# Front of a hybrid diffusion step: later small loads, a latent tile begun by token halves, norm weights inside the rotation tables

## The chip, the cores and the metric

One core of a Trainium2 chip runs the whole program in one launch. The metric is the device time of one execution in microseconds (us), lower is better; it is compared as a median of several runs. TensorE (PE) does the matrix products and the transposes, VectorE (DVE) and ScalarE (ACT) the elementwise work, GpSimd (POOL) some elementwise work and some DMA issues, SyncE (SP) the other DMA issues.

## What is computed

The reference is one layer of a trunk with 1024 latent tokens and 256 prompt tokens, D_MODEL = 1024, all in fp32. Cut to the part that the change touches:

```python
mod = silu(cond) @ w_ada + b_ada                  # cond = c for latent tokens, c_ctx for prompt
sh1, sc1, g1, sh2, sc2, g2 = split(mod, 6)
h = rms_norm(x, norm_mix_w) * (1 + sc1) + sh1
z = h @ w_in                                      # hq, hf_f, hf_b, hi, hg, aq, ak, av, gl
q = rms_norm(aq by heads of 64, q_norm_w)         # 8 query heads
k = rms_norm(ak by heads of 64, k_norm_w)         # 2 key heads
if latent:                                        # 2-D axial rotary positions
    q, k = axial_rope(q), axial_rope(k)           # per half: x1*cos - x2*sin, x1*sin + x2*cos
    k, v = concat(cache_k, k), concat(cache_v, v)
# then attention, a gated linear recurrence (HGRN), gates, an output projection, an MLP, norms
```

## The kernel before, in words

**Numbers and tiles.** Every fp32 operand of a product is kept as a pair, a rounded high part and the rest: ACT copies the high part, DVE subtracts (`split`, lines 277 and 278). One product is three matmuls: high by high, high by low, low by high. Tokens are tiled as t=0 and t=1 (512 latent tokens, 4 blocks of 128 each) and t=2 (256 prompt tokens, 2 blocks). The width 1024 is cut into KC=8 chunks kc of 128. A *step* z(t,kc) below is the matmuls of chunk kc for tile t onto the 512 columns of `w_in` that hold k, v and half of the queries (`front_z`, lines 553 to 562): for 4 blocks 8 matmuls with the high part of h (L558, L559), then 4 with its low part (L562).

**The front (lines 577 to 633).** `norm1_rows` (224 to 251) loads the token rows `xr`, takes sums of squares (ACT L241, for t=0 half of them on DVE L237 and L238), raises the mean to the power -0.5 on POOL (`rst`, L247) and scales the rows on DVE (L250). `front_ada(j)` (518 to 534), j=0..3, loads eight 256 KB pieces `wa` of `w_ada` and does 64 narrow matmuls (L530) for the shift and scale columns of two chunks; its result is copied by ACT (`ev`, L533), and `front_late(j)` (536 to 545) transposes it on PE (L539) and makes `modc` and `s` (`s1`) on DVE (L543, L544). `norm1_tr` (253 to 257) transposes the rows of one chunk into a PSUM tile `ps_t`, of which there are two, and `norm1_col` (259 to 271) reads it: ACT makes the high part `hs` (L265), ACT or for every third chunk DVE the unrounded value `xnb` (L270, L268), DVE the low part `hs` (L271). `front_w(kc)` (547 to 551) loads and splits a row block `wst` of `w_in`.

For t=0 the columns come two chunks at a time, between the steps z(0,kc). From step 7 on, columns run AHEAD=3 steps before their step: ahead of z(0,7) stand the 12 transposes of chunks 0 to 2 of t=1.

**What follows a tile.** `front_done` copies the banks out by pairs of blocks (`kve` L442, `qe` L448). `front_prep` calls `kv_consume` and `q_consume` for each pair: `qk_norm` (390 to 416) squares (ACT L394), reduces (DVE L396), adds EPS (DVE L165), takes the power on POOL (`qrst`, L166), multiplies by it (`qn`, DVE L399) and by the norm weight `qwb` or `kwb` (DVE L400). For latent pairs the rotation follows: `qa` = `qn` by `cosb`, one DVE op for each block (L408); `qb` = `qn` with its halves exchanged by `sinb`, two POOL ops for each block (L413); their sum on POOL for queries and DVE for keys (L415). The transposes of rotated keys (`k_stack`, L424) and queries (L473) are put on PE some way behind, by a clock of due times (`DUE`, `due`, `flush`). `cache_kv` does the same for the cached keys and values (`ck`, `cv`). After the front `z_tok(AQ)` multiplies the other half of the queries; its first matmul is L325.

**Order.** The order on PE is that of the program text. On the other engines a scheduler orders the instructions by priority: `norm1_col` and the evacuations have a raised one (`high_priority(offset=600)`). Buffers come from rings: the rows `xr` from ring X of 20, the loads `wa` and `wst` from other rings, and a load waits until its buffer is free.

**Small loads (lines 116 to 149).** `small` loads short vectors as rows and transposes them into `cols` (L129, L130). SP issues `c` and `c_ctx` as its first two; POOL issues the rest at the start: `b_ada`, `norm_mix_w`, `norm_ffn_w`, `final_norm_w`, `hgrn_lb_logits`, `qwb`, `kwb`, `hnb` and two masks.

## Time and profile before

| what | us |
|---|---|
| median of 3 runs (2054.65 to 2057.73) | 2055.32 |
| the profiled execution | 2055.24 |
| its span in the trace | 2053.1 |
| PE busy in the span | 2012.3 |
| DVE busy | 1405.3 |
| ACT busy | 938.5 |
| POOL busy | 546.1 |

The mean granted clock of PE is 0.998 of full. The page's busy times are sums over the whole span; the front is its first 104 us, and the rows that matter are those that a view of this stretch gives: what PE waited for, by line, and the instructions of each engine in order of time. In a row of the timeline stand the start, the duration, the engine, the line, the operation with "out<-in", the shape, the count, and in brackets how long the engine was idle before it and what released it. A group of several instructions in one row has the duration from its first start to its last end.

### The profile page before, as it was taken

The page shows a single profiled execution, that of the slowest core. Times are in us where ns is not written, and L with a number is a line of the kernel's source. Part 1 is how long each engine was busy: PE and PEld are TensorE (multiplying, and loading weights), DVE is VectorE, ACT ScalarE, POOL GpSimd, SP SyncE. Part 2 cuts the span into 40 slices and gives each one's busy share as a digit, 9 for nine tenths or more (in the row PEclk, how much of TensorE's full clock was granted, in tenths as well). Part 3 has the DMA queues.
Part 4 walks back from the last instruction along what each step waited for, and adds up shares of the span by engine and source line. Part 5 has one row for each costly group of instructions (what it writes and reads, how often), then busy time and mean ns, then how long its engine had stood idle before and what let it go on. Part 6 is the DMA issues. An engine that isn't in the chain of part 4 may idle for free.

```text
span 2053.1 us, 33691 instructions
## 1 busy us (share of the span) xinstructions
PE 2012.3 (98%) x12470; PEld 1736.1 (85%) x12470; DVE 1405.3 (68%) x2655; ACT 938.5 (46%) x1906; POOL 546.1 (27%) x566
## 2 busy tenths in 40 slices
PE   6899999999999999999999999999999999999998
PEld 5798889988889988888888889998888888888886
DVE  4876776777776788779254634886666666577686
ACT  4735555555555423332321335655455544333443
POOL 1473333333332265545112101222122110000130
PEclk9999999999999999999999999999999999999999
DMA  9453220322211455455544533864444489455764
GB/s 309 150 187 97 78 77 27 108 86 78 78 45 65 132 175 167 153 173 159 196 138 149 180 113 116 259 186 151 157 147 157 145 292 361 148 159 176 232 238 142
DMA packets 220052, 317.38 MB, mean 155 GB/s; under 512 B 18504, under 2 KB 139168, under 8 KB 219888
## 3 DMA queue, kind: packets, MB, share of 16 engines
q1 hardware_dynamic: 207216, 275.05, 41.7%
q0 software_dynamic: 12672, 40.18, 5.5%
q8 instruction: 98, 1.61, 0.3%
q14 instruction: 66, 0.54, 0.1%
HBM read 229.43 MB, written 85.74 MB: 154 GB/s over the span
## 4 chain that ended last, share of the span: by engine, by line
PE 62%; DVE 2%; issue 1%; ACT 0%; DMA 0%; POOL 0%; POOLq 0%; ACTq 0%; DVEq 0%
PE ps_g L308 5%; PE ps_g L309 5%; PE ps_g L310 5%; PE ps_g L1614 2%; PE ps_g L1616 2%; PE ps_g L1615 2%; PE ps_s L1460 2%; PE ps_s L1461 2%; PE ps_s L1459 2%; PE ps_s L1614 2%; PE ps_s L1615 2%; PE ps_s L1616 2%; PE ps_t L1614 2%; PE ps_t L1615 2%; PE ps_t L1616 2%; PE ps_s L308 2%
## 5 line engine op out<-in xcount | busy, mean ns | idle before, releaser
L308 PE MATMUL ps_g<-hs,wsp 128*128 128x512 f32 (+1 forms) x896 | 322.2, 360 | 1.1 <-DVE adas L186 1.0
L310 PE MATMUL ps_g<-hs,wsp 128*128 128x512 f32 (+1 forms) x896 | 309.3, 345 | 0.0
L309 PE MATMUL ps_g<-hs,wsp 128*128 128x512 f32 (+1 forms) x896 | 309.1, 345 | 0.0
L716 POOL TENSOR_SCALAR pexp<-pexp,rs 128x512 f32<-128x512 f32 (+1 forms) x104 | 171.5, 1655 | 364.8 <-ACT pTh L741 210.6
L277 ACT ACTIVATE wsp<-wraw 128x1024 fp32r<-128x1024 f32 x110 | 109.7, 997 | 276.6 <-PE ps_g L309 82.8
L278 DVE TENSOR_TENSOR wsp<-wraw,wsp 128x1024 fp32r<-128x1024 f32 x110 | 139.9, 1272 | 114.8 <-ACT wsp L277 114.4
L308 PEld LDWEIGHTS ps_g<-hs,wsp 128*128 128x128 f32 x896 | 169.6, 189 | 22.3 <-issue 4.6
L310 PEld LDWEIGHTS ps_g<-hs,wsp 128*128 128x128 f32 x896 | 169.3, 189 | 21.5
L309 PEld LDWEIGHTS ps_g<-hs,wsp 128*128 128x128 f32 x896 | 169.9, 190 | 14.8
L741 ACT ACTIVATE pTh<-ps_t 128x512 fp32r<-128x512 f32 x200 | 118.4, 603 | 124.5 <-PE ps_t L738 124.4
L277 ACT ACTIVATE ah<-ar 128x640 fp32r<-128x640 f32 (+1 forms) x112 | 80.9, 723 | 185.1 <-PE ps_g L1615 102.3
L698 DVE TENSOR_REDUCE mx<-ps_s 128x1 f32<-128x512 f32 (+1 forms) x208 | 137.1, 663 | 37.7 <-PE ps_s L697 36.9
L708 ACT ACTIVATE pexp<-ps_s,ngm 128x512 f32<-128x512 f32 (+1 forms) x208 | 137.4, 670 | 43.7 <-DVE ngm L702 42.9
L278 DVE TENSOR_TENSOR ah<-ar,ah 128x640 fp32r<-128x640 f32 (+1 forms) x112 | 93.1, 832 | 77.2 <-ACT ah L277 76.1
L742 DVE TENSOR_TENSOR pTl<-ps_t,pTh 128x512 fp32r<-128x512 f32 x200 | 135.9, 681 | 14.1 <-ACT pTh L741 13.9
L697 PE MATMUL ps_s<-Kl,Ql 128*128 128x512 f32 (+1 forms) x416 | 130.7, 411 | 0.7 <-ACT pexp L708 0.7
L738 PE MATMUL ps_t<-ident,pexp 128*128 128x128 f32 x800 | 120.8, 273 | 3.3 <-DVE pTl L742 1.8
L325 PE MATMUL ps_g<-wsp,hs 128*128 128x256 f32 x400 | 115.9, 290 | 0.0
L327 PE MATMUL ps_g<-wsp,hs 128*128 128x256 f32 x400 | 112.9, 282 | 0.0
L326 PE MATMUL ps_g<-wsp,hs 128*128 128x256 f32 x400 | 112.5, 281 | 0.0
L754 PE MATMUL ps_g<-pTl,Vl 128*128 128x256 f32 x400 | 105.9, 287 | 4.0 <-DVE pTl L742 4.0
L738 PEld LDWEIGHTS ps_t<-ident,pexp 128*128 128x128 f32 x800 | 93.6, 140 | 14.1 <-issue 4.0
(421 smaller groups left out, 5395.2 us busy)
## 6 DMA issues: line engine op xcount, KB each, us to landing
ar<-AF SPq DMA_DIRECT2D x112, 320.0 KB, 3.2
wraw<-in_w_ff SPq DMA_DIRECT2D x32, 1024.0 KB, 6.1
wr<-in_w_ff SPq DMA_DIRECT2D x128, 256.0 KB, 4.4
wraw<-in_w_in SPq DMA_DIRECT2D x18, 1024.0 KB, 5.7
wraw<-in_w_ada SPq DMA_DIRECT2D x16, 1024.0 KB, 5.6
AF<-a POOLq DMA_DIRECT2D x48, 256.0 KB, 2.7
AF<-t POOLq DMA_DIRECT2D x48, 256.0 KB, 2.4
wa<-in_w_ada SPq DMA_DIRECT2D x32, 256.0 KB, 5.8
```

What stands on the lines that cost most here:

```text
L277: s_.activation(hi, raw, AF.Copy)
L278: return v.tensor_tensor(lo, raw, f32(hi), op=ALU.subtract)
L308: pe.matmul(out, hi[:, k, :], mh, start=(first and k == 0), stop=False)
L309: pe.matmul(out, hi[:, k, :], ml, start=False, stop=False)
L310: pe.matmul(out, lo[:, k, :], mh, start=False, stop=(last and k == kcs - 1))
L697: pe.matmul(pq[:, 0:n], self.qh[:, q0:q0 + P], K[self.g][var][self.kts[i]], start=(var == 0), stop=(var == 1))
L698: v.tensor_reduce(self.mx[j][:, i:i + 1], pq[:, 0:n], axis=AX.X, op=ALU.max)
L708: s_.activation(e[:, 0:n], self.ps.pop((j, i))[:, 0:n], AF.Exp, bias=self.mx[j], accum_out=self.sm[j][:, i:i + 1])
L716: NORM[(i + j) % len(NORM)].tensor_scalar(x, x, self.rs[j], None, op0=ALU.mult)
L738: pe.transpose(pt[:, a, j * P:(j + 1) * P], self.Ps[j][i][:, b * P:(b + 1) * P], ident)
L742: v.tensor_tensor(lo, pt, f32(hi), op=ALU.subtract)
L1614: pe.matmul(bank, ph, wh, start=first and i == 0, stop=False, **more)
```

## The change

1. **Small loads.** `c` and `c_ctx` are issued by POOL, ahead of `b_ada`; SP starts with `xr`. `qwb` and `kwb` are issued by POOL behind the row powers of t=0. `hnb`, the masks and the three vectors that are needed later (`load_rest`) are issued by POOL at step 7, behind the row powers of t=1. The two loads of `state_hgrn` go behind `sinb` on SP.
2. **Row norms by halves.** `norm1_rows` takes a list of blocks: blocks 0,1 and blocks 2,3 have a power each. Half of the squares of every tile (i=1) are one DVE op with an accumulated sum. For t=1 and t=2 the squares are gated behind named instructions (`issue_after`).
3. **First columns.** The 8 transposes of chunks 0 and 1 of t=0 stand inside the 64 matmuls of `front_ada(0)`, ahead of k=6. The splits of the first two row blocks of `w_in` are ordered behind `ev` and the scales.
4. **Tile t=1.** z(0,7) is cut: 8 matmuls, then the transposes of chunks 0 and 1 for blocks 0,1 of t=1, then its last 4. z(1,0) and z(1,1) run for blocks 0,1 first, then the transposes for blocks 2,3, z(1,0) for blocks 2,3, the 12 transposes of chunks 2 to 4, and z(1,1) for blocks 2,3. The evacuation of t=0 is ordered by pairs between these. Later columns run 3 to 5 steps ahead; `cache_kv` comes four steps later.
5. **Rotation.** `rope_tables` makes four tables on POOL with 6 ops, the cosines and sines times the norm weight of queries and of keys. For rotated pairs the multiplication L400 is gone, `qa` is one DVE op and `qb` one POOL op with a reversed axis.

```diff
-    small((("c", 8), ("c_ctx", 8)), CC, sp)()
+    small((("c", 8), ("c_ctx", 8)), CC, g_)()
...
+                    if i == 1:
+                        jk = S(name="sqv")
+                        v.scalar_tensor_tensor(jk, xt[i], 1.0, xt[i], op0=ALU.mult, op1=ALU.mult, accum_out=acc)
...
+    def rope_tables():
+
+        cosq, sinq = S((P, 8, 64), name="cosb"), S((P, 8, 64), name="sinb")
+        for c, sn, w in ((cosq, sinq, qwb), (cosb, sinb, kwb)):
+            g_.tensor_tensor(c, cosb, w.unsqueeze(1).broadcast_to([P, 8, 64]), op=ALU.mult)
...
+            for s in range(2):
+                g_.tensor_tensor(out[:, :, :, s], in_[:, :, :, s], w4[:, :, 1 - s].unsqueeze(1).broadcast_to([P, 8, 2, 16]), op=ALU.mult)
...
-        for bb in range(2):
-            blk = blk0 + bb
-            v.tensor_tensor(qa[:, bb], qn[:, bb], cosb[:, blk].unsqueeze(1).broadcast_to([P, nh, 64]), op=ALU.mult)
...
-            for s in range(2):
-                g_.tensor_tensor(bv[:, :, :, s], nv[:, :, :, 1 - s],
-                                 sv[:, :, s].unsqueeze(1).broadcast_to([P, nh, 2, 16]), op=ALU.mult)
+        cw, sw = [x[:, blk0:blk0 + 2] for x in rope_w[nh]]
+        v.tensor_tensor(qa, qn, cw.unsqueeze(2).broadcast_to([P, 2, nh, 64]), op=ALU.mult)
...
+        g_.tensor_tensor(bv, qv[:, :, :, :, ::-1], sv, op=ALU.mult)
...
+            if mid and k == 6:
+                mid()
...
+    norms = [norm1_rows(0, bs, rows_n[0]) for bs in ((0, 1), (2, 3))]
+    wa0 = ada_load(0)
...
+    with tc.issue_after(norms[1][0].ins):
+        load_qk_w()
...
+    lates = front_ada(0, wa0, lambda: pts.extend(norm1_tr(0, rows_n[0], kc) for kc in range(2)))
+    with tc.issue_after(lates[2].ins):
+        s_.activation(w_row(0)[0], raws[0], AF.Copy)
...
-        if idx == KC:
+        if idx == KC + 4:
             cache_kv()
...
+            front_z(t, kc, banks, first_half)
...
+        elif idx == KC:
+            for k in range(2):
+                front_z(1, k, banks, None, (0, 1))
+            for k in range(2):
+                norm1_tr(1, rows_n[1], k, half[k], (2, 3))
+                made = norm1_col(1, k, half[k], (2, 3))
+            with tc.issue_after(made.ins):
+                evs += front_done(0, banks0, (1,))
+            _, f = norm1_rows(2, (0, 1), rows_n[2], {(b, i): [low[0] if i else made] for b in range(2) for i in range(2)})
...
+            front_z(1, 0, banks, None, (2, 3))
...
+                with tc.issue_after(norms[1][0].ins):
+                    rope_w.update(rope_tables())
...
+        if idx == KC - 1:
+            with tc.issue_after(norms[1][0].ins):
+                lbs = load_rest()
```

Three places show what this does to the order of the instructions. In the rows below, "x3" is a count of like instructions in a row.

PE, from the end of z(0,6) on, before: all of the first three chunks of t=1 are transposed (`xr`, x12) ahead of z(0,7), whose first matmuls are L558 and L559.

```order
L562 MATMUL ps_s<-wsp,hs 128x512 x3
L562 MATMUL ps_g<-wsp,hs 128x512
L256 MATMUL ps_t<-ident,xr 128x128 x12
L558 MATMUL ps_s<-wsp,hs 128x512
L559 MATMUL ps_s<-wsp,hs 128x512
```

The same engine now, first from inside z(0,7), then from the end of z(1,1) for blocks 0,1 to the 12 transposes of chunks 2 to 4 (L580, L581 and L586 are the lines of a step, L258 the row transposes).

```order
L581 MATMUL ps_g<-wsp,hs 128x512
L258 MATMUL ps_t<-ident,xr 128x128 x4
L586 MATMUL ps_s<-wsp,hs 128x512 x3
L586 MATMUL ps_g<-wsp,hs 128x512
L580 MATMUL ps_g<-wraw,hs 128x512
```

```order
L586 MATMUL ps_g<-wraw,hs 128x512 x2
L258 MATMUL ps_t<-ident,xr 128x128 x4
L580 MATMUL ps_s<-wraw,hs 128x512
L581 MATMUL ps_s<-wsp,hs 128x512
L580 MATMUL ps_s<-wraw,hs 128x512
L581 MATMUL ps_s<-wsp,hs 128x512
L586 MATMUL ps_s<-wraw,hs 128x512 x2
L258 MATMUL ps_t<-ident,xr 128x128 x12
```

Four of the twelve transposes have moved from ahead of z(0,7) into it, four behind the first halves of z(1,0) and z(1,1).

PE at the first transposes of rotated keys (`qa`, x2), before: they stand behind z(1,5), ahead of two transposes of prompt rows.

```order
L562 MATMUL ps_g<-wsp,hs 128x512 x2
L562 MATMUL ps_s<-wsp,hs 128x512 x2
L424 MATMUL ps_t<-ident,qa 128x128 x2
L256 MATMUL ps_t<-ident,xr 128x128 x2
L558 MATMUL ps_g<-wsp,hs 128x512
```

Now they stand behind z(1,3), and six row transposes follow: the last chunk of t=1 and the first of the prompt.

```order
L586 MATMUL ps_g<-wraw,hs 128x512 x2
L586 MATMUL ps_s<-wraw,hs 128x512 x2
L439 MATMUL ps_t<-ident,qa 128x128 x2
L258 MATMUL ps_t<-ident,xr 128x128 x6
L580 MATMUL ps_g<-wsp,hs 128x512
```

The first rotated keys are asked for two steps of z(1,kc) earlier.

POOL from the row powers of t=1 (`rst`) on, before: the next is the power of the prompt rows, then the powers and rotations of the first pair.

```order
L247 TENSOR_TENSOR rst<-mm,mexp 128x4
L247 TENSOR_TENSOR rst<-mm,mexp 128x2
L166 TENSOR_TENSOR qrst<-ms,mexp 128x4
L413 TENSOR_TENSOR qb<-qn,sinb 128x4x16 x4
L166 TENSOR_TENSOR qrst<-ms,mexp 128x8
```

Now the six ops of the tables and the six late loads stand between these.

```order
L247 TENSOR_TENSOR rst<-mm,mexp 128x2 x2
L402 TENSOR_TENSOR cosb<-cosb,qwb 128x512
L406 TENSOR_TENSOR sinb<-sinb,qwb 128x16x16 x2
L145 DMA hnb<-in_hgrn_norm_w 128x128
L147 DMA mask_106<-const_masks 128x128
L147 DMA mask_107<-const_masks 128x128
L124 DMA rows<-in_norm_ffn_w 8x128
L124 DMA rows<-in_final_norm_w 8x128
L124 DMA rows<-in_hgrn_lb_logits 16x128
L402 TENSOR_TENSOR cosb<-cosb,kwb 128x512
L406 TENSOR_TENSOR sinb<-sinb,kwb 128x16x16 x2
L247 TENSOR_TENSOR rst<-mm,mexp 128x2
```

The power of the prompt rows, and every later power of queries and keys, has moved behind twelve more instructions of POOL.

More of the change, by code (lines that the diff above doesn't have):

```diff
@@ L100, in dma @@
     def dma(out, in_):
-        sp.dma_start(out=f32(out), in_=f32(in_))
+        return sp.dma_start(out=f32(out), in_=f32(in_))
     def store(out, in_):
@@ L222, in build, with norm1_rows @@
     hT = [[None] * KC for _ in range(3)]
-    def norm1_rows(t):
+    def norm1_rows(t, blocks, xs, behind=None):
         t0, n, cond = TT[t]
-        xs = []
+        b0, nb = blocks[0], len(blocks)
         ss = T(8, "ss")
         rst = T(4, "rst")
-        nb = NB[t]
-        for b in range(nb):
+        for b in blocks:
             xt = load_x(t0 // P + b)
             for i in range(2):
-                acc = ss[:, 2 * b + i:2 * b + i + 1]
-                if t == 0 and i == 1:
-                    jk = S(name="sqv")
-                    v.tensor_tensor(jk, xt[i], xt[i], op=ALU.mult)
-                    v.tensor_reduce(acc, jk, axis=AX.X, op=ALU.add)
-                else:
-                    jk = S(name="sq")
-                    s_.activation(jk, xt[i], AF.Square, accum_out=acc)
+                acc = ss[:, 2 * (b - b0) + i:2 * (b - b0) + i + 1]
+                with ExitStack() as after:
+                    if behind:
+                        for x in behind[b, i]:
+                            after.enter_context(tc.issue_after(x.ins))
+                    if i == 1:
+                        jk = S(name="sqv")
+                        v.scalar_tensor_tensor(jk, xt[i], 1.0, xt[i], op0=ALU.mult, op1=ALU.mult, accum_out=acc)
+                    else:
+                        jk = S(name="sq")
+                        s_.activation(jk, xt[i], AF.Square, accum_out=acc)
             xs.append(xt)
@@ L559, in front_z, with front_done @@
             pe.matmul(banks[b], mh[:, off:off + P], wl, start=False, stop=False)
-        for b in range(NB[t]):
+        if mid:
+            mid()
+        for b in blocks or range(NB[t]):
             off = b * P
             pe.matmul(banks[b], ml[:, off:off + P], wh, start=False, stop=(kc == KC - 1))
-    def front_done(t, banks):
+    def front_done(t, banks, pairs=None):
         out = []
-        for p2 in range(NB[t] // 2):
+        for p2 in pairs or range(NB[t] // 2):
             b2 = banks[2 * p2:2 * p2 + 2]
@@ L621, in build, with first_half @@
-        front_z(t, kc, banks)
+            scales = front_late((kc + 1) // 2, lates)
+        if idx < KC - 1 or idx > KC + 1:
+            front_z(t, kc, banks)
+        elif idx == KC - 1:
+            half = []
+            def first_half():
+                nonlocal made
+                for k in range(2):
+                    half.append(norm1_tr(1, rows_n[1], k, None, (0, 1)))
+                    made = norm1_col(1, k, half[k], (0, 1))
+            front_z(t, kc, banks, first_half)
+            with tc.issue_after(low[0].ins):
+                for _, f in norms:
+                    f(1)
+        elif idx == KC:
+            for k in range(2):
+                front_z(1, k, banks, None, (0, 1))
+            for k in range(2):
+                norm1_tr(1, rows_n[1], k, half[k], (2, 3))
[3 more added lines that the diff above has]
+            _, f = norm1_rows(2, (0, 1), rows_n[2], {(b, i): [low[0] if i else made] for b in range(2) for i in range(2)})
+            f(0)
+            f(1)
+            front_prep(evs)
+            front_z(1, 0, banks, None, (2, 3))
+        else:
+            front_z(1, 1, banks, None, (2, 3))
@@ L622, in build @@
         if cols_next:
             for i in (1, 2):
-                norm1_col(0, kc + i, pts[i - 1])
+                made = norm1_col(0, kc + i, pts[i - 1])
                 due(0.6)
-        elif t == 0 and kc < KC - 2:
+            if kc == KC - 3:
+                late = [made, scales]
+                gates = {(b, i): late if b else [lates[2]] if i == 0 else [] for b in range(4) for i in range(2)}
+                norms = [norm1_rows(1, bs, rows_n[1], gates) for bs in ((0, 1), (2, 3))]
+                for _, f in norms:
+                    f(0)
+                dma(cosb, C["cos"].rearrange("(b p) d -> p b d", p=P))
+                loaded = dma(sinb, C["sin"].rearrange("(b p) d -> p b d", p=P))
+                with tc.issue_after(norms[1][0].ins):
+                    rope_w.update(rope_tables())
+        elif idx < KC - 2:
@@ L944, in prep @@
                 self.st = cp.tile([P, P], F32, tag="s0", name="s0", bufs=2)
-                dma(self.st, I["state_hgrn"][d, h])
+                with tc.issue_after(loaded.ins):
+                    dma(self.st, I["state_hgrn"][d, h])
         def keys_t(self):
```

151 lines of the change are left out of this document (85 added, 66 removed).

## The prediction

> **What bounds the kernel now.** I read the waits of PE first, cut to the first 160 us. A row says which line waited, which instruction released it, the total, the count and the longest.
>
> ```profile
> PE ps_g L530 <- DVE qwb L148: 8.9, 1, 8.9
> PE ps_s L558 <- ACT hs L265: 2.1, 1, 2.1
> PE ps_t L256 <- ACT xnb L270: 2.0, 2, 1.2
> PE ps_t L256 <- DVE xr L250: 1.4, 1, 1.4
> PE ps_t L256 <- DVE kT L278: 1.2, 2, 0.8
> ```
>
> Behind the front PE has almost nothing to wait for, as the busy times by stretch show (PE is the first number behind the length):
>
> ```profile
> 104.00:604.00 500.00, 492.94 (x3458) 442.01 (x3457) 358.45 (x743) 273.60 (x636) 185.45 (x128) 1.00 0.27 87
> ```
>
> So PE bounds the kernel, and a microsecond saved ahead of the first matmul of AQ (L325) is saved at the end. I therefore follow one engine from landmark to landmark: the first step, the end of z(0,6), z(1,2), AQ.
>
> **Term 1, the start.** The timeline of PE, ACT and DVE between the last load of the first `wa` pieces and the first step, and below them `hs` of the second round, j=1:
>
> ```profile
> 20.10 0.63 PE L530 MATMUL ps_g<-wa,ada_l 128*32 128x128 f32 x12 [0.33 <-DMA wa<-in_w_ada]
> 24.00 0.50 PE L558 MATMUL ps_s<-wraw,hs 128*128 128x512 f32 x1 [2.08 <-ACT hs L265]
> ...
> 20.75 0.63 ACT L277 ACTIVATE wraw<-wst 128x512 fp32r<-128x512 f32 x1 [9.36 <-DMA wst<-in_w_in]
> 21.28 0.26 ACT L533 ACTIVATE ev<-ps_g 128x128 f32<-128x128 f32 x1
> ...
> 21.41 1.39 DVE L278 TENSOR_TENSOR wsp<-wst,wraw 128x512 fp32r<-128x512 f32 x2 [2.13 <-ACT wraw L277]
> 22.91 0.17 DVE L544 SCALAR_TENSOR_TENSOR s<-modc,cols 128x4 f32<-128x4 f32 x1
> ...
> 32.09 0.78 ACT L265 ACTIVATE hs<-ps_t,modc,s 128x512 fp32r<-128x512 f32 x1 [1.26 <-DVE s L544]
> ```
>
> The last piece lands at 20.1, the first step starts at 24.0: 3.9 us. In that time ACT splits a row of `w_in` ahead of `ev`, and DVE two rows ahead of `modc` and `s`; the new order puts both behind. At j=1, where nothing stands in front, ACT is idle for 1.26 between `ev` and `hs`, so `ev` ends at 30.83 and `hs` at 32.87: 2.04 us, of which some 0.4 are eight transposes ahead of L539 that are now inside the ada matmuls. With `ev` (0.26), the last narrow matmuls (0.3) and hand-overs (0.2) I take 2.4 instead of 3.9: 1.5 us.
>
> The landing itself moves too. DMA by stretches (last numbers: granted clock, DMA share, GB/s), the POOL queue's share in the first 22 us, and SP's first issue of rows:
>
> ```profile
> 9.00:10.00 1.00, 0.00 (x0) 0.00 (x0) 0.49 (x3) 0.72 (x2) 0.00 (x0) 1.00 1.08 247
> 10.00:11.00 1.00, 0.00 (x0) 0.00 (x0) 0.97 (x2) 0.33 (x1) 0.00 (x0) 1.00 1.06 203
> 13.00:14.00 1.00, 0.00 (x0) 0.00 (x0) 0.97 (x2) 0.00 (x0) 0.00 (x0) 1.00 1.07 356
> ...
> q0 software_dynamic: 320, 0.31, 10.0%
> ...
> 1.55 1.78 SPq L101 DMA_DIRECT2D xr<-in_x_sample  x4
> ```
>
> The engines are full from 9 us on, but move 203 to 247 GB/s while small packets run and 356 after. POOL's queue takes 10% of 22 us, 2.2 us. By its bytes some three quarters of it (`hnb`, masks, late vectors) now come after 50 us: 1.5 us sooner for `wa`. SP's two rows no longer stand ahead of `xr`: issue at 0.7 instead of 1.55, 0.8 us. Landing 17.8, first step 20.2: **+3.8 us**. Low bound: if the small packets only filled gaps, +1.5. A half-clock stretch comes with the wait ahead of the first step:
>
> ```profile
> 26.00:27.00 1.00, 1.00 (x4) 0.76 (x3) 0.82 (x2) 0.00 (x0) 0.00 (x0) 0.50 1.04 357
> ```
>
> It lasts some 3.4 us and costs 1.7. With a wait of 2 us left I keep it; if it goes, +1 more. The Trainium skill ("TensorE: Matmul & The Clock Gate", section "What's actually happening") has the half rate follow an idle window of about 3.4 us, on a window that runs free of the kernel. The trace agrees in the length of the slow stretch; by that rule alone a coin decides whether it stays.
>
> PE gains 3.8 on loads that gain 2.3. The third round's last piece comes twenty pieces (256 KB at 356 GB/s, 0.74 us each) after the first round's, at 32.6; its matmuls start at 33.2, 3.8 before the row below, so the later loads stay covered, barely.
>
> ```profile
> 36.97 1.96 PE L530 MATMUL ps_g<-wa,ada_l 128*32 128x128 f32 x64
> ```
>
> **Term 2, the begin of t=1.** PE and ACT rows, in order of time on each engine:
>
> ```profile
> 53.63 0.39 PE L562 MATMUL ps_g<-wsp,hs 128*128 128x512 f32 x1
> 55.40 1.86 PE L256 MATMUL ps_t<-ident,xr 128*128 128x128 f32 x8 [1.38 <-DVE xr L250]
> 62.69 0.48 PE L558 MATMUL ps_g<-wraw,hs 128*128 128x512 f32 x1
> 65.53 0.60 PE L256 MATMUL ps_t<-ident,xr 128*128 128x128 f32 x4
> 69.07 0.48 PE L558 MATMUL ps_g<-wraw,hs 128*128 128x512 f32 x1
> ...
> 59.05 1.44 ACT L265 ACTIVATE hs<-ps_t,modc,s 128x512 fp32r<-128x512 f32 x2
> 61.18 0.38 ACT L442 ACTIVATE kve<-ps_s 128x256 f32<-128x256 f32 x1
> 61.46 0.38 ACT L448 ACTIVATE qe<-ps_s 128x256 f32<-128x256 f32 x1
> 79.25 0.56 ACT L265 ACTIVATE hs<-ps_t,modc,s 128x256 fp32r<-128x256 f32 x1
> 79.70 0.57 ACT L270 ACTIVATE xnb<-ps_t,modc,s 128x256 f32<-128x256 f32 x1
> ```
>
> From the end of z(0,6) at 54.0 to z(1,2) at 69.07 it takes 15.1 us, of which 3.0 are waits (1.38 for the rows, 1.15 for `xnb`, 0.46). A step of four blocks takes 2.84 (62.69 to 65.53), of two 1.42. Now, counted from the end of z(0,6) as 0: the first 8 matmuls of z(0,7) 1.9, four transposes 0.45, the last four 0.9, z(1,0) and z(1,1) for two blocks 2.8, four transposes: 6.4, without a wait, for the rows are scaled by halves. There the cover ends. ACT makes three half columns (0.45 each), four evacuations (0.28 each), a square with its sum (0.75), values of V (0.4) and chunk 2 (two ops at 0.67): 5 us, so `ps_t` is free for chunk 4 only at 11.3. Its transposes, chunk 3's two ops and their low part add 2.9: z(1,1) is through at 14.2, z(1,2) starts at 14.6. The stall at the start of t=1 moves into the 12 transposes: **+0.5 us**, bounds 0 and +3.0.
>
> **Term 3, z(1,2) to AQ.** The step durations above and AQ's start give the transposes; DVE and POOL rows price the chain that the first rotated keys need:
>
> ```profile
> 104.35 0.39 PE L325 MATMUL ps_g<-wsp,hs 128*128 128x256 f32 x1
> ...
> 59.64 1.66 DVE L250 TENSOR_SCALAR xr<-xr,rst 128x512 f32<-128x512 f32 x4
> 72.05 0.67 DVE L396 TENSOR_REDUCE qss<-sq 128x8 f32<-128x512 f32 x1
> 72.65 0.41 DVE L399 TENSOR_TENSOR qn<-kve,qrst 128x256 f32<-128x256 f32 x1
> 72.98 0.68 DVE L400 TENSOR_TENSOR qn<-qn,qwb 128x512 f32<-128x512 f32 x1
> ...
> 58.38 0.70 POOL L247 TENSOR_TENSOR rst<-mm,mexp 128x2 f32<-128x2 f32 x1 [3.65 <-DVE mm L246]
> 80.56 1.28 POOL L415 TENSOR_TENSOR qa<-qa,qb 128x512 f32<-128x512 f32 x1
> ...
> L413 POOL TENSOR_TENSOR qb<-qn,sinb 128x128 f32<-128x128 f32 x32 | 19.6, 642 | 12.2 <-DVE qn L400 10.5 <-DVE ms L165 1.4 <-DVE qa L415 0.4
> L145 POOL DMA_DIRECT2D mask<-const_masks x2 | 1.1, 563 | 0.0
> ...
> 80.63 1.50 DVE L415 TENSOR_TENSOR qa<-qa,qb 128x256 f32<-128x256 f32 x1 [0.22 <-POOL qb L413]
> ```
>
> Before: 69.07 to 104.35 is 35.3 us; six steps at 2.84 and eight at 1.42 are 28.4, waits 2.04 (`kT` 1.2, `xnb` 0.85), and 43 transposes the rest, 4.8, or 0.11 each. Now 41 stand there (a key pair falls behind AQ's first matmuls): +0.25.
>
> The waits grow. POOL's tables (two ops like L415 at 1.3, four of half that size, estimated 0.9) and six loads (0.56 each) take 9.6 us from the row powers of t=1 at about 0.3, so POOL is free at about 9.9; but the power of the prompt rows, ahead of every later power, waits for the prompt's second square on ACT, which stands behind chunk 2: 12.4, done at 13.3. Behind it DVE runs in order four scales (1.66), then four low parts, an unrounded value, four reductions, two `qn`, a cosine multiplication and the sum of the keys: eight of 512 elements at 0.60 (72.05 to 72.65), four of 256 at 0.33, three small ones: 6.9. The keys are ready at about 22.1, PE asks for them behind z(1,3) at 20.5: 1.6 us. Six row transposes stand next, and their buffer comes free behind the split of these keys, which on DVE follows a multiplication of 0.60 and one of 0.33: 0.95 where it was 0.37. Later waits, for which nothing changes by name, I keep at 0.8 of 1.67. Sum 3.35 against 2.04, less the 0.25: **-1.05 us**. Bounds: no wait for the keys, +0.85; the rival below.
>
> The single POOL op for `qb` of 512 elements (with its reversed axis) replaces four of 0.64; I take 1.6, between one like L415 (1.28) and the four together (2.57).
>
> **Sum.** 3.8 + 0.5 - 1.05 = 3.25 us off the profiled execution of 2055.24, which stands 0.08 below the median: 2052.0. About 0.2%, 4.1 us, is what a measurement of this kernel can tell from no change.
>
> **The rivals.**
>
> *The keys are not late.* If DVE's order has gaps that I filled and the keys are there at 20.5, the wait of 1.6 and 0.58 of the next go: 5.4 us, 2049.8 (2048.8 without the half clock). For it: DVE has no multiplication L400 now and one cosine op instead of two. Against: the prompt's squares stand late in ACT's order. 0.30.
>
> *Nothing comes from the loads.* The pieces are bound by their own 256 KB each, and the landing stays at 20.1. Then 1.5 + 0.5 - 1.05 = 0.95: 2054.3. Against it speak the 203 GB/s at a full share. 0.10.
>
> *POOL holds DVE.* When POOL's sum ran at 80.56 for 1.28, DVE's sum of the keys took 1.50 for two ops' worth of 0.42. If each long POOL op with two full operands does so, the key tables (3.1) and the rotation of the first two pairs (0.9, 1.6, 1.3 each) hold DVE 10.7 us; with half of the second pair hidden 8.8, and DVE is on the path from 9.9 on. 8.8 - 3.25 = 5.5 us slower: 2060.8. It decides as soon as DVE loses over 3.25 us there. Against it: powers and the four short `qb` ops run beside DVE ops of normal length. 0.14.
> The Trainium skill ("SBUF — State Buffer", section "SBUF: two separate sides") states it as a rule: the port pair of both engines is a lock, held for a whole instruction. The row at 80.63 agrees.
>
> **How the numbers follow.** Forecast 0.46, the rivals 0.30, 0.10, 0.14. The range: low is the first rival without the half clock and without the later waits, some 2046.5; high is the forecast with half of the 10.7 held, 2057.4, and half of the 2.3 by which the landing may move less: 2058.5. The full last rival lies outside. Faster by over 0.2% (under 2051.2) is nearly all of the first rival (0.26) and the forecast's lower third (0.13): 0.39. Slower is most of the last rival: 0.12. The rest is 0.49.
>
> **What would show it.** First step at 20.2, not 24.0; end of z(0,6) at 50.2; a wait of some 2 us inside the 12 transposes; PE waiting about 1.6 for `qa` behind z(1,3); L325 at about 101.1. I am wrong if the first step stays past 22.5, if DVE rows beside POOL's long ops double, or if L325's shift does not reach the end.

## The result, and the profile after

The changed kernel takes 2061.14 us (median of 9 runs, 2058.82 to 2062.31), the kernel before 2055.32 (9 runs, 2054.19 to 2057.73): a ratio of 1.0026, 95% interval 1.0015 to 1.0036. It is slower by 0.26%, where 2052.0 was forecast, and lies above the range of 2046.5 to 2058.5. The profiled execution took 2058.82, the fastest of the nine, with a span of 2057.0; the differences below are made against its trace and so explain 3.6 us (3.9 of span) of the 5.8 between the medians.

| start of | before | forecast | after |
|---|---|---|---|
| first step | 24.00 | 20.2 | 19.59 |
| end of z(0,6) | 54.0 | 50.2 | 49.35 |
| z(1,2) | 69.07 | 64.8 | 68.94 |
| AQ, first matmul (L325, now L333) | 104.35 | 101.1 | 107.80 |
| attention's first score matmul (L697, now L782) | 157.4 | | 164.2 |
| its last | 693.7 | | 698.5 |
| span | 2053.1 | | 2057.0 |

So 4.65 us are gained by the end of z(0,6), all of it is lost again by z(1,2), 3.6 more are lost up to AQ and 3.4 behind it. Of these the attention gives back 2.0 and the rest of the program 0.9.

**The start.** The timeline of PE after: the first step, with the wait before it in brackets.

```profile
19.59 0.50 PE L580 MATMUL ps_s<-wraw,hs 128*128 128x512 f32 x1 [1.28 <-ACT hs L270]
```

The stretches of the DMA that moved 247 and 203 GB/s before (last number):

```profile
9.00:10.00 1.00, 0.13 (x1) 0.16 (x1) 0.81 (x5) 0.52 (x3) 0.72 (x1) 1.00 1.09 374
10.00:11.00 1.00, 0.20 (x1) 0.02 (x1) 1.00 (x4) 0.72 (x2) 0.00 (x0) 1.00 1.09 346
```

And the POOL queue's share of the first 22 us (packets, MB, share), which was 10.0%:

```profile
q0 software_dynamic: 192, 0.10, 2.4%
```

The small packets had cost the big pieces their rate, as forecast; the half-clock stretch behind the first step is gone too. In return the second round of `wa` pieces (j=1) has not all landed when PE comes to it: its 64 narrow matmuls take 2.5 us, where they take 1.95 once their loads have landed, with a short wait for a load (0.15, at 24.41) and one of 0.51 for `ev` behind them.

**The waits of PE**, first 160 us (line that waited, releaser, total, count, longest). Of the rows that are new or have grown, those behind the first step:

```profile
PE ps_s L586 <- DVE hs L276: 2.8, 1, 2.8
PE ps_t L488 <- POOL qa L430: 2.4, 1, 2.4
PE ps_t L258 <- DVE kT L286: 2.2, 2, 1.5
...
PE ps_g L559 <- ACT ev L554: 0.9, 2, 0.5
PE ps_g L586 <- DVE hs L276: 0.7, 1, 0.7
```

The two rows with DVE's `hs` (L276) are low parts of the first chunks of t=1: a wait that stood nowhere before. PE's timeline there, from z(0,7) and the first halves of z(1,0) and z(1,1) to z(1,2), which starts at 68.94, and behind it:

```profile
54.17 0.73 PE L586 MATMUL ps_g<-wraw,hs 128*128 128x512 f32 x2 [0.73 <-DVE hs L276]
...
61.15 1.22 PE L586 MATMUL ps_s<-wraw,hs 128*128 128x512 f32 x2 [2.79 <-DVE hs L276]
...
64.77 1.11 PE L258 MATMUL ps_t<-ident,xr 128*128 128x128 f32 x4 [0.69 <-ACT xnb L275]
...
66.53 0.63 PE L580 MATMUL ps_s<-wraw,hs 128*128 128x512 f32 x1
66.96 0.63 PE L581 MATMUL ps_s<-wsp,hs 128*128 128x512 f32 x1
...
68.94 0.78 PE L580 MATMUL ps_g<-wraw,hs 128*128 128x512 f32 x1
...
70.71 0.39 PE L581 MATMUL ps_s<-wsp,hs 128*128 128x512 f32 x1
70.93 0.39 PE L580 MATMUL ps_s<-wraw,hs 128*128 128x512 f32 x1
```

From the end of z(0,6) to z(1,2) it takes 19.6 us where 14.6 were forecast. The matmuls start 0.43 us apart at 66.5 and 0.22 apart at 70.7: from within the wait of 2.79 PE's granted clock is half of full, 59.84 to 70.08, for 10.2 us. What DVE and POOL do meanwhile, DVE first (L252 scales a row, L276 makes a low part, L402 and L406 are the tables):

```profile
51.00 1.37 DVE L252 TENSOR_SCALAR xr<-xr,rst 128x512 f32<-128x512 f32 x1
52.29 0.96 DVE L252 TENSOR_SCALAR xr<-xr,rst 128x512 f32<-128x512 f32 x1
53.17 0.95 DVE L276 TENSOR_TENSOR hs<-xnb,hs 128x256 fp32r<-128x256 f32 x1
54.95 4.75 DVE L252 TENSOR_SCALAR xr<-xr,rst 128x512 f32<-128x512 f32 x4
60.69 0.41 DVE L276 TENSOR_TENSOR hs<-xnb,hs 128x256 fp32r<-128x256 f32 x1
...
50.66 1.42 POOL L402 TENSOR_TENSOR cosb<-cosb,qwb 128x512 f32<-128x512 f32 x1
52.05 1.79 POOL L406 TENSOR_TENSOR sinb<-sinb,qwb 128x256 f32<-128x256 f32 x2
54.38 1.06 POOL L147 DMA_DIRECT2D mask<-const_masks  x2
57.16 1.38 POOL L402 TENSOR_TENSOR cosb<-cosb,kwb 128x512 f32<-128x512 f32 x1
58.51 1.76 POOL L406 TENSOR_TENSOR sinb<-sinb,kwb 128x256 f32<-128x256 f32 x2
```

A scale took 0.48 before, and four in a row 1.66, each beginning 0.4 behind the last. The first one beside a table op takes 1.37 and ends at 52.37, 0.3 after POOL's cosine op (52.08). The low part of 0.41 (60.69) takes 0.95 beside the sines and ends at 54.12, 0.3 after them (53.84). Four scales at 54.95 take 4.75. DVE gets on when POOL's op is through, and PE waits for DVE.
The Trainium skill ("SBUF — State Buffer", section "Who interferes with whom") has DVE and GpSimd share one pair of ports as an exclusive lock, held for the whole instruction by whichever began first; it names the scaling op in its fast mode, and two-operand ops with both inputs in SBUF. The rows agree for the table ops: DVE's ends follow POOL's. They do not agree for POOL's small power before them, beside which the first two scales (from 50.05) ran at their length.

**The keys and AQ**, PE after:

```profile
77.25 0.41 PE L439 MATMUL ps_t<-ident,qa 128*128 128x128 f32 x2 [1.60 <-DVE qa L430]
79.57 0.44 PE L258 MATMUL ps_t<-ident,xr 128*128 128x128 f32 x2 [1.48 <-DVE kT L286]
...
116.06 0.66 PE L488 MATMUL ps_t<-ident,qa 128*128 128x128 f32 x4 [2.39 <-POOL qa L430]
```

The key wait is 1.60, as forecast, and half clock follows it (80.3 to 83.7, a loss of 1.7 us). Behind AQ's start there were waits of 0.3 and 0.2 before; now one of 2.39, behind which the clock stays full.

### The profile page after: what moved, and what is told of

The parts are those of the page before. It is cut to its first block, busy times and chain, and to the rows that moved or that the text cites. A ratio compares the mean times of both kernels' runs of the same rounds, so it can differ in the third digit from the quotient of the medians.

```text
span 2057.0 us, 33642 instructions
## 1 busy us (share of the span) xinstructions
PE 2013.9 (98%) x12470; PEld 1738.2 (85%) x12470; DVE 1404.4 (68%) x2650; ACT 935.9 (45%) x1897; POOL 545.2 (27%) x540
## 4 chain that ended last, share of the span: by engine, by line
PE 90%; DVE 4%; DMA 2%; ACT 1%; issue 1%; POOL 1%; SPq 0%; DVEq 0%; POOLq 0%; ACTq 0%
PE ps_g L316 8%; PE ps_g L318 8%; PE ps_g L317 8%; PE ps_s L782 4%; PE ps_t L823 4%; PE ps_g L1700 2%; PE ps_g L1702 2%; PE ps_g L1701 2%; PE ps_g L839 2%; PE ps_s L1546 2%; PE ps_s L1547 2%; PE ps_s L1545 2%; PE ps_g L838 2%; PE ps_s L1700 2%; PE ps_s L1702 2%; PE ps_s L1701 2%
## 5 line engine op out<-in xcount | busy, mean ns | idle before, releaser
L317 PEld LDWEIGHTS ps_g<-hs,wsp 128*128 128x128 f32 x896 | 170.0, 190 | 14.6
L286 DVE TENSOR_TENSOR ah<-ar,ah 128x640 fp32r<-128x640 f32 (+1 forms) x112 | 92.2, 824 | 76.2 <-ACT ah L285 75.8
L782 PE MATMUL ps_s<-Kl,Ql 128*128 128x512 f32 (+1 forms) x416 | 130.0, 411 | 0.0
L333 PE MATMUL ps_g<-wsp,hs 128*128 128x256 f32 x400 | 116.0, 290 | 0.0
```

Of the source, the lines that this page charges most:

```text
L286: return v.tensor_tensor(lo, raw, f32(hi), op=ALU.subtract)
L317: pe.matmul(out, hi[:, k, :], ml, start=False, stop=False)
L782: pe.matmul(pq[:, 0:n], self.qh[:, q0:q0 + P], K[self.g][var][self.kts[i]], start=(var == 0), stop=(var == 1))
```

## The experiments

The theory (A): POOL's table ops hold DVE's row scales and low parts at the begin of t=1; the stall brings half clock, and both together eat the start's gain. Its rivals: the late loads, which POOL issues at the same place, do it; the new one-op rotation does it; PE's order asks for the first rotated keys too early, whatever DVE does; the gain at the start would not have reached the end in any case. Each expectation below says in its own words which of them it tells apart. Ratios are to the kernel before on the same chip. In all but e8, e9 and e10 the halving of `hnb`, a DVE op that waits for a late load, is also ordered behind a low part at the end of the front. In the change it takes DVE 0.21 us at 60.55, just ahead of the low part that PE waits for.

### e1: without the tables

```diff
-        for c, sn, w in ((cosq, sinq, qwb), (cosb, sinb, kwb)):
...
+        return {4: (cosb, sinb), 2: (cosb, sinb)}
```

The norm weights of queries and keys are left out of the computation here.

> The changed kernel without the six table ops on POOL; the rotation uses the plain cosines and sines, so the norm weights of rotated queries and keys are left out. The multiplication of hnb is pinned to the end of the front on DVE, so that it can't wait there for its load. Theory A (POOL's table ops hold DVE's row scales and low parts at the begin of t=1): the third and fourth scale take 0.4 instead of 1.37 and 0.96 us, the wait of 0.7 us for the first low part goes, the wait of 2.8 us for the second low part falls to 1.5 or less, and z(1,2) starts 15.5 us or less behind the end of z(0,6) instead of 19.7; the time falls by 4 us or more, to 2057 or below. Theory B (the halves' order itself is late, whoever runs beside it): z(1,2) still 19 us behind, time within 1 us of the changed kernel's 2061.

2054.87 us, ratio 0.9999 (0.9990 to 1.0008). DVE's scales are back at their length, with the late loads still issued by POOL there, and the two waits for low parts are gone; z(1,2) starts at 65.00, where 64.8 was forecast:

```profile
50.45 1.85 DVE L252 TENSOR_SCALAR xr<-xr,rst 128x512 f32<-128x512 f32 x4
55.22 1.67 DVE L252 TENSOR_SCALAR xr<-xr,rst 128x512 f32<-128x512 f32 x4
```

But PE, there earlier, now waits longer for the keys (3.15 instead of 1.60), with half clock from 75.8 to 82.7, and AQ starts at 106.06. The tables cost some 6 us at the end, and even without them the kernel is no faster than before. (The profiled execution has half clock behind the first step as well, 21.2 to 24.6.)

### e2: the late loads later

```diff
-        if idx == KC - 1:
-            with tc.issue_after(norms[1][0].ins):
+        if idx == 2 * KC - 1:
+            with tc.issue_after(added[0].ins):
                 lbs = load_rest()
```

`added` is the sum of the second pair's queries on POOL.

> The changed kernel with the six late loads of POOL moved behind the rotation of the second pair (and the multiplication of hnb pinned to the end of the front on DVE). The tables now follow each other without the loads between. Theory A with loads harmless: DVE's scale that took 1.58 us beside the loads is held by the key tables instead, and POOL is done 3.4 us earlier, so DVE's second four scales still take 3 us or more in all but the low parts of the second half (at 60.7) come about 1 to 2 us earlier: 2059 to 2060. Theory A2 (issuing loads holds DVE as much as the tables): the four scales, 4.75 us now, fall by the 1.6 us that the loads hold; 2058 or below. Theory B: within 0.7 us of 2061.

2056.4 us, ratio 1.0001 (0.9993 to 1.0010). The scales are still held, the second four less:

```profile
50.66 3.20 DVE L252 TENSOR_SCALAR xr<-xr,rst 128x512 f32<-128x512 f32 x4 [0.54 <-POOL rst L247]
...
56.09 2.62 DVE L252 TENSOR_SCALAR xr<-xr,rst 128x512 f32<-128x512 f32 x4
```

The waits for low parts are 0.79 and 0.48, z(1,2) starts at 66.54. Without the loads between them the key tables run sooner, and are over before most of the second half's work on DVE. So the loads can matter through the place to which they push the key tables. But I had expected 2059 to 2060 from that, and 2058 or below if issuing loads holds DVE; the time fits the second, and the scale of 1.58 that stood beside the loads in the change is gone here too. This run does not tell the two apart. The kernel is some 5 us faster than the change, without being faster than before.

### e3: the tables on DVE

```diff
-            g_.tensor_tensor(c, cosb, w.unsqueeze(1).broadcast_to([P, 8, 64]), op=ALU.mult)
+            v.tensor_tensor(c, cosb, w.unsqueeze(1).broadcast_to([P, 8, 64]), op=ALU.mult)
...
+            with tc.issue_after(low[0].ins):
+                rope_w.update(rope_tables())
```

All six ops move, behind a low part of t=1's second half.

> The changed kernel with the six table ops on DVE, placed behind the low parts of the second half of t=1 (and the multiplication of hnb pinned as in the run without tables); the result is complete. Theory A: the begin of t=1 is as short as without tables (z(1,2) at most 16 us behind the end of z(0,6)), the tables cost DVE about 2.6 us behind it, of which at most 2 show as a later wait for the first rotated keys: 2055 to 2058. Theory B: 2061 or more, since DVE has more to do.

2054.91 us, ratio 0.9996 (0.9987 to 1.0005). DVE, and the keys on PE:

```profile
50.77 1.83 DVE L252 TENSOR_SCALAR xr<-xr,rst 128x512 f32<-128x512 f32 x4 [0.41 <-POOL rst L247]
55.19 1.67 DVE L252 TENSOR_SCALAR xr<-xr,rst 128x512 f32<-128x512 f32 x4
59.28 0.68 DVE L402 TENSOR_TENSOR cosb<-cosb,qwb 128x512 f32<-128x512 f32 x1
...
73.75 0.66 PE L439 MATMUL ps_t<-ident,qa 128*128 128x128 f32 x2 [3.30 <-DVE ms L163]
```

The work is the same as in the change and only its engine differs: z(1,2) at 64.26, 4.7 sooner, and no wait for a low part. From z(0,6) it takes 13.6 us, a little under the 14.6 forecast. The long op costs DVE 0.68, where it cost POOL 1.42 and held one of DVE's scales for 0.9. The key wait is 3.30, half clock lies at 73.6 to 80.4, and AQ starts at 104.83, 0.5 later than in the kernel before: the 4.8 us by which z(1,2) is sooner than there are spent on the wait for the keys and the half clock behind it.

### e4: the rotation of before

```diff
+        v.tensor_tensor(qn.rearrange("p b h d -> p (b h) d"), qn.rearrange("p b h d -> p (b h) d"),
+                         wb.unsqueeze(1).broadcast_to([P, n, 64]), op=ALU.mult)
...
-        g_.tensor_tensor(bv, qv[:, :, :, :, ::-1], sv, op=ALU.mult)
+        for bb in range(2):
```

No tables, and the weights, `qa` and `qb` as before; all else as in the change.

> The changed kernel with the rotation as before: no tables, the multiplication by the norm weight and two cosine ops on DVE, four short POOL ops for each pair (hnb pinned as above). Theory A: the begin of t=1 as without tables, the chain of the rotated keys some 1 us longer on DVE; 2055 to 2058, and about 1 us above the run without tables. If the long single POOL ops of the rotation cost as much as the tables (they hold DVE's sum and scalings), it is faster than the run without tables. Theory B: 2061 or more.

2061.35 us, ratio 1.0025 (1.0015 to 1.0034), as slow as the change. The begin is as theory A has it (z(1,2) at 63.78, AQ at 104.44, as before), but then, in AQ, PE and POOL:

```profile
124.32 0.90 PE L481 MATMUL ps_t<-ident,qa 128*128 128x128 f32 x3 [4.79 <-POOL qa L423]
...
119.18 3.24 POOL L421 TENSOR_TENSOR qb<-qn,sinb 128x128 f32<-128x128 f32 x4
```

Four short ops per pair of queries (3.24) come too late for the new place of the query transposes: a wait of 4.79, half clock from within it (121.6 to 128.4), the first score matmul at 166.0. I had expected this kernel to be fast. What was lost ahead of z(1,2) in the change is lost behind AQ here, so a late POOL costs time in AQ too, and the one-op rotation is not the culprit; it is needed.

### e5: the start alone

The new start and the later loads, with the t=1, prompt, tables and rotation of before:

```diff
-        if idx == KC + 4:
+        if idx == KC:
             cache_kv()
...
-        cols_next = idx < KC - 1 and kc % 2 == 1
+        cols_next = t == 0 and kc % 2 == 1 and kc < KC - 1
```

> The kernel before with the start of the change alone: c and c_ctx on POOL, qwb and kwb behind the row powers, the six late loads behind the rotation of the second pair, t=0's norm by halves, its first transposes inside the ada matmuls, and the splits of the first rows behind ev and the scales. Tile t=1, the rotation and the due times are those of before. If term 1 of the prediction is right and what is saved ahead of AQ is saved at the end: first step at 19.6 to 20.6 instead of 24.0, end of z(0,6) near 50, then the waits of before, 2051 to 2052. Rival (the gain is given back where rows of t=1, paced by loads, come no earlier): end of z(0,6) near 50 but z(1,2) not before 67.5: 2054 or more.

2055.62 us, ratio 0.9997 (0.9988 to 1.0006). The first step starts at 18.66, 5.3 sooner, and AQ at 102.72, only 1.6 sooner. On the way PE waits 2.04 for `ev`, which stands behind t=1's squares on ACT, then 1.67 for `xnb`, with half clock from 55.2 to 58.6; and in AQ:

```profile
45.36 0.33 PE L556 MATMUL ps_g<-ident,ev 128*128 128x128 f32 x1 [2.04 <-ACT ev L551]
147.07 0.89 PE L485 MATMUL ps_t<-ident,qa 128*128 128x128 f32 x4 [2.61 <-POOL qa L425]
```

So the rival on the start held in this order: when PE comes sooner and ACT and POOL do not, it waits for them. A sooner start needs an order of t=1 in which ACT and POOL are sooner too; e9 shows below that it then keeps a part.

### e6 and e7: tables on DVE, rotated keys and queries asked for later

```diff
-        pending.append((due(DUE[0]), late))
+        pending.append((due(DUE[0]) + (6.0 if kgv == 1 else 0.0), late))
...
-            pending.append((due(DUE[1]), late))
+            pending.append((due(DUE[1]) + (6.0 if g == 1 and pr < 2 else 0.0), late))
```

e7 is e3 with these due times; e6 has 4.0 in place of 6.0.

> The run with the tables on DVE, and the transposes of the rotated keys and queries of the first two pairs one to two steps later on PE (due times plus 4). If the late keys cost that run its gain (3.3 us of waiting behind z(1,3), and the half clock from 74 to 81 that follows, some 3 us): the wait falls below 1 us, but the queries, now behind z(1,5), may be waited for by up to 3 us; 2050 to 2053. Rival (the waits only move to the next item in the queue): 2054 or more.

> As the run before, due times plus 6: keys behind z(1,5), queries behind z(1,6), as in the kernel before. No wait of over 1 us behind z(1,3), no half clock after it: AQ starts near 98 to 100, 2048 to 2050. Rival as before: 2054 or more.

e6: 2052.78 us, ratio 0.9986 (0.9977 to 0.9995); waits of 1.1 to 1.2 for keys and queries and half clock at 79.9 to 83.3 remain, AQ at 102.17. e7: 2050.27 us, ratio 0.9971 (0.9961 to 0.9982), faster than both the kernel before and the change. Its longest waits between 14 and 160 us:

```profile
PE ps_t L258 <- ACT xnb L275: 2.3, 3, 1.1
PE ps_t L258 <- DVE kT L286: 2.3, 2, 1.5
```

Ten microseconds of it (PE's busy time and instructions first, the granted clock third from the end):

```profile
58.00:68.00 10.00, 8.20 (x46) 6.51 (x45) 9.92 (x30) 9.58 (x24) 1.62 (x1) 1.00 0.49 154
```

And the same ten of the change:

```profile
58.00:68.00 10.00, 6.53 (x22) 4.98 (x21) 8.38 (x24) 6.87 (x21) 3.16 (x4) 0.59 0.57 155
```

46 matmuls instead of 22, and no half clock anywhere in e7 between 58 and 98. AQ starts at 99.51, 4.8 sooner than in the kernel before, the first score matmul at 153.3 (4.1 before), and the span is 4.4 shorter: here what was saved ahead of AQ is there at the end.

### e8: the due times alone

The change with the edit of e7's diff, its tables left on POOL.

> The changed kernel, tables on POOL as it has them, with only the due times of the first two pairs plus 6. Waits for keys behind z(1,3) (1.6 and 1.5 us) and the half clock from 80 to 84 (1.7 us) go, the stall and the half clock at the begin of t=1 stay: 2056 to 2058. If the stall at the begin of t=1 is the whole loss and the late keys cost nothing: 2060 or more.

2055.76 us, ratio 0.9999 (0.9990 to 1.0008). The key wait is gone, the wait for the low part, 2.79 in the change, is not:

```profile
61.26 1.22 PE L586 MATMUL ps_s<-wraw,hs 128*128 128x512 f32 x2 [2.82 <-DVE hs L276]
```

Half clock comes with it for 3.4 us here (60.7 to 64.1), where the change has 10.2, and again behind a wait of 2.1 for `kT` (84.6 to 88.0).

Medians of the four kernels that cross the two edits:

| | due times of the change | six later |
|---|---|---|
| tables on POOL | 2061.1 | 2055.8 |
| tables on DVE | 2054.9 | 2050.3 |

The tables' place is worth 6.2 and 5.5 us, the due times 5.4 and 4.6: two separate causes of about the same size, and they add. (The lower row also has the halving of `hnb` ordered, 0.21 us of DVE.)

### e9: the start of before, in e7

```diff
+    _, f = norm1_rows(0, (0, 1, 2, 3), rows_n[0])
+    f(0)
+    f(1)
+    lates = front_ada(0)
+    front_w(0)
+    front_w(1)
```

The small loads are issued at the start again, too.

> The run with the tables on DVE and the due times plus 6 (2050.3), with the start of before put back: c and c_ctx on SP, all small loads at the beginning, t=0's norm in one piece, its first transposes behind the ada matmuls, no order for the first splits. If what the start saves reaches the end once nothing behind it swallows it: end of z(0,6) near 54 and 2054 to 2055. Rival (the start is worth little at the end, as the run with the start alone suggests): 2052 or less.

2053.15 us, ratio 0.9986 (0.9977 to 0.9994). Here the first step waits for its column as before:

```profile
23.83 0.50 PE L585 MATMUL ps_s<-wraw,hs 128*128 128x512 f32 x1 [2.08 <-ACT hs L275]
```

Against e7 the start is worth 2.9 us at the end, of 4.5 at the first step (19.29 in e7), 2.8 at the end of z(0,6) and 2.8 at AQ. The kernel is faster than I had expected here: part of the start's gain is lost, all of it ahead of z(0,3), and the rest is kept. From the first step to z(0,3) it takes 14.3 us here and 16.0 in e7, whose second and third round of narrow matmuls take 2.3 and 2.5 us in place of 1.95, since their loads have not landed when PE is there. And with the small loads back at the start the DMA moves 312, 168 and 213 GB/s from 9 to 12 us, so they are what cost the big pieces their rate.

### e10: the row scales on ACT

```diff
+                if t == 1:
+                    s_.activation(x, x, AF.Copy, scale=rst[:, b - b0:b - b0 + 1])
...
-            with tc.issue_after(low[0].ins):
+            with tc.issue_after(made.ins):
                 for _, f in norms:
                     f(1)
```

The tables stay on POOL; the second half's scales are gated behind a column's op on ACT in place of a low part.

> The changed kernel with the eight row scales of t=1 on ACT instead of DVE; tables and loads on POOL where it has them. If only DVE is held by POOL's long ops: ACT's scales take 0.6 us each beside the tables, the waits for the low parts (0.7 and 2.8 us) fall to 1 us or less together, though the low parts themselves (0.95 instead of 0.42) are still held; late keys stay; 2055 to 2058. If ACT is held as well, its scales take over 0.9 us and the time stays above 2060.

2060.18 us (2056.14 to 2061.81), ratio 1.0020 (1.0011 to 1.0029). ACT beside the tables, and POOL's sines:

```profile
49.84 2.57 ACT L253 ACTIVATE xr<-xr,rst 128x512 f32<-128x512 f32 x4 [1.20 <-POOL rst L247]
...
51.70 1.43 POOL L409 TENSOR_TENSOR sinb<-sinb,qwb 128x256 f32<-128x256 f32 x2
```

Four scales take ACT 2.57 and 2.58 in the two halves, 0.64 each, beside POOL's ops or not: of the two engines it is DVE alone that is held. POOL's pair of sines took 1.43, where it took 1.79 next to a busy DVE, so each holds the other. z(1,2) comes at 66.22. The time did not follow, and missed the 2055 to 2058 that I had expected: ACT, now later with `hs` and `xnb`, is waited for instead (1.1 to 1.5 each), and the key wait is 3.05. The profiled execution was the fastest of the eleven, 4 us under the median, and what the slower ones lost is not seen.

### e11: late loads behind the rotation, in e7

e7 with e2's diff.

> The run with the tables on DVE and the due times plus 6, with the six late loads behind the rotation of the second pair as well. If issuing loads on POOL holds DVE: the row scales of t=1 take 1.66 instead of 1.83 us, no more than 0.5 us in all, since ACT sets the pace there: 2049.5 to 2050.5. If the loads cost more than the traces show (transfers, queue): 2049 or less.

2050.76 us, ratio 0.9976 (0.9967 to 0.9985): no difference to e7. Without tables beside them the late loads on POOL cost nothing that can be measured.

### e12: the tables on POOL for nobody

e7, whose tables are on DVE, with six more ops of the same shapes at the change's place on POOL (one ahead of the late loads and five behind, where the change has three and three), into a tile that nobody reads:

```diff
+                    idle = S((P, 8, 64), name="cosb")
+                    for w in (qwb, kwb):
+                        g_.tensor_tensor(idle, cosb, w.unsqueeze(1).broadcast_to([P, 8, 64]), op=ALU.mult)
...
```

> The run with the tables on DVE and the due times plus 6 (2050.3), and in addition the six table ops on POOL where the changed kernel has them, behind the row powers of t=1 (one of them ahead of the six loads, five behind), writing into a tile that nobody reads. Nothing waits for their results, so all that they can cost is what POOL's running holds up beside it. If POOL holds DVE while it runs: row scales and low parts of t=1 take 0.9 us and more beside the six ops, PE waits 2 us or more for a low part, and the time rises by 3 to 6 us, to 2053 to 2056. If the changed kernel lost its time by waiting for tables, and not by POOL's running: within 1 us of 2050.3.

2052.95 us, ratio 0.9984 (0.9975 to 0.9993), 2.7 over e7. No result of these ops is awaited, and yet on DVE and PE:

```profile
50.48 2.80 DVE L252 TENSOR_SCALAR xr<-xr,rst 128x512 f32<-128x512 f32 x4 [0.54 <-POOL rst L247]
55.30 2.62 DVE L252 TENSOR_SCALAR xr<-xr,rst 128x512 f32<-128x512 f32 x4
57.84 1.50 DVE L276 TENSOR_TENSOR hs<-xnb,hs 128x256 fp32r<-128x256 f32 x1
...
59.39 0.73 PE L586 MATMUL ps_s<-wraw,hs 128*128 128x512 f32 x2 [1.16 <-DVE hs L276]
```

In e7 the same eight scales took 1.83 and 1.67. That POOL's ops hold DVE's scales and low parts, which depend on none of them, is shown by these rows. The time shows less: the intervals of the two ratios (e7 up to 0.9982, e12 from 0.9975) overlap, and 2.7 is a little under the 3 to 6 expected and half of the 5.5 between e8 and e7. The trace has a reason for the small size: PE's wait is 1.16, where I had expected 2 or more, and no half clock follows it, so from the end of z(0,6) to z(1,2) it takes 15.0 us, 1.4 more than in e7 and 3.4 less than in e8. Part of the 2.7 can also come from DVE's own key tables, which here overwrite cosines and sines that POOL still reads.

## Why the prediction was wrong

**Term 1 was right in its causes, and its number at z(0,6) owes something to luck.** First step at 19.59 (forecast 20.2), 4.4 sooner, 4.65 at the end of z(0,6), against 3.8. Both reasons are in the trace: the DMA's rate, and the splits behind `ev` and `s`. Behind the first step two errors nearly cancel. The half clock that I kept went in this execution (it came in the profiled ones of e1, e10, e11 and e12), which is worth 1.6: from the first step to z(0,1) it takes 7.3 us before and 5.8 in e9, which has the old start without half clock. But the change takes 7.1: the loads that I took to be covered are not, in the second round already, where I had looked at the third alone.

**Term 2 failed, and with it the forecast.** z(1,2) starts 19.6 behind the end of z(0,6), where 14.6 stood. The first step that failed is the pricing of the tables: "POOL is free at about 9.9" counted six ops and six loads as time of POOL's queue alone, which nobody awaits yet. What they cost is DVE's time beside them. e1 and e3, without them on POOL, need 14.3 and 13.6 for the same stretch, so the rest of the term was sound, down to the row scales by halves.

How the 19.6 come about, against e3's 13.6: the four waits are 0.73 + 0.44 + 2.79 + 0.69 = 4.65, in e3 2.23, so 2.4 more. Then the clock: from 61.15 to 68.94 PE works 7.1 us (7.79 less the wait of 0.69); in e3 the same instructions take from 58.50 to 64.26 less 1.79 of waits, 4.0. That is 3.1 more. 0.5 is left over. So over half of the loss is not the stall, but the half clock behind it, which I priced at the start and nowhere else. Not every run pays as much for it: e8, with the same wait, has 3.4 us of half clock there. The granted clock of all runs points the same way. It was 0.9952 on the mean of the change's nine runs and 0.9974 on that of the 32 runs of the kernel before that stand beside e1; one minus the clock, times the span, is 9.8 and 5.4 us, an estimate by which 4.4 of the 5.8 us between the medians are lost clock. In e8 it is 0.9968, in e7 0.9986.
The Trainium skill ("TensorE: Matmul & The Clock Gate", section "What's actually happening") has the half rate set in after an idle window of about 3.4 us and end after a busy one. Here the longest single wait was 2.79 us and the slow stretch 10.24, three such windows: idle time of less than a window, next to little work, was enough.

**Term 3 failed as well, and its waits came out by luck.** The key wait is 1.60 (1.6), the split behind it 1.48 (0.95), the later one 0.71 (0.8): 3.79 against 3.35. Two stretches of half clock, 1.7 behind the keys and 0.5 left over from term 2, make up the rest of the 3.6 us by which AQ falls behind, counted from z(1,2). But here PE asks for the keys late, because of term 2. In e1, where z(1,2) starts as forecast, PE asks 20.5 behind the end of z(0,6), as forecast too, and the prompt's power is through at 13.3, again as forecast; but the keys come at 23.6, not at 22.1. So the wait of 1.6 should have been 3.15, and the half clock behind it, 6.8 us or a loss of 3.4, stood in no term. The step that failed here is the 6.9 us of DVE for the chain of the keys (13.3, 1.66 and 6.9 add up to 21.9, not 22.1): two of its ops run beside POOL's rotation, the multiplication `qn` (1.20 in e1, 0.69 alone) and the sum of the keys (1.29, alone 0.42), and these lose 1.4 us. The change has the same rows:

```profile
75.83 1.27 DVE L430 TENSOR_TENSOR qa<-qa,qb 128x256 f32<-128x256 f32 x1
...
75.55 1.26 POOL L429 TENSOR_TENSOR qb<-qn,sinb 128x512 f32<-128x512 f32 x1
```

So it is POOL holding DVE a second time. In e7 the rotation still holds DVE (two `qn` multiplications take 1.35 and 1.22), but with the later due times PE does not wait for it.

**The premise** that a microsecond saved ahead of AQ is saved at the end holds in e7 and failed in the change, in e4 and in e5: query transposes in AQ then wait for POOL (2.39, 4.79, 2.61), since POOL is late by its own queue. The other way, some 2 us come back within the attention: from first to last score matmul it takes 536.3 us before and 534.3 after. What gives them back is open.

**The rival that came true** had the mechanism, and the rows behind it were in the profile of before. Its number (2060.8) is near by luck: it adds up 8.8 us of held DVE from 9.9 on and no half clock, where much of the loss is half clock and the first hold comes sooner. I gave it 0.14, because powers and short ops of POOL ran beside DVE ops of normal length. For the powers this holds; for the short rotation ops I misread the profile of before, in which they lengthen DVE's ops already (two cosine ops of 0.42 take 1.28):

```profile
82.86 1.28 DVE L408 TENSOR_TENSOR qa<-qn,cosb 128x256 f32<-128x256 f32 x2
...
82.20 2.26 POOL L413 TENSOR_TENSOR qb<-qn,sinb 128x128 f32<-128x128 f32 x4 [0.36 <-DVE qa L415]
```

The sum of the keys at 80.63, which I called two ops' worth, is a single op of 0.42 that took 1.50. And I let the rival decide only from 9.9 on, at the key tables and the rotation. It decided at the first table, 1.3 us behind the end of z(0,6), on two kinds of DVE ops that I had not looked at in this respect: row scales and low parts.

**Open.** In the change and in e8 one scale took 1.58 while POOL only issued loads (54.95 in the change), in e10 one low part 1.46, in e12 one 0.98; in e1 and e3 DVE runs at its length beside the same issues, and e11 shows no cost. Whether issuing holds DVE at times is not settled. Nor is the spread of 2 to 7 us between runs of one kernel, which is as large as the effects here; the medians carry the comparisons.

## What to carry to other kernels

Price an elementwise op that is moved to POOL by what DVE runs at the same time, not by POOL's own queue: an op that nobody awaits can still stop the engine that everybody awaits. Where PE is nearly full, allow for half clock behind a stall of two or three microseconds as well: here it cost as much again, though not every stall brought it. And when a front is made to start sooner, move every later request (due times) along with the engine that makes the operand, or the gain waits there.

## What the runs showed of the hardware

POOL's table ops (128x512 at 1.42 us, 128x256 at about 0.9) hold a DVE scale of 0.48 us until some 0.3 us after their own end, and its rotation op of 128x512 holds a sum of 0.42 for 1.27, while POOL's small powers do not (the first two scales, from 50.05 on, ran at their length beside one), and ACT is not held at all (0.64 with the tables beside it and without). POOL pays too: 1.79 for two ops next to a busy DVE, 1.43 without.

PE's half clock came in stretches of 3.4, 6.8 or 10.2 us, in which step matmuls start 0.43 instead of 0.22 us apart. All eight waits of 2.6 us and more behind the first 16 us of the fourteen profiles brought one (2.79 in the change, 2.82 in e8, 3.05 to 4.79 in e1, e3, e4 and e10, 2.72 in e4, 2.61 in e5), but not of the same length: 10.2 us behind 2.79, 3.4 behind 2.82. Of five waits between 2.0 and 2.4 two did (2.08 in the kernel before and in e8), and three did not (2.39 in the change, 2.04 in e5, 2.08 in e9).
